# One PSUM pool of seven banks in place of pools of two, two and three, in a decoder-layer kernel on one Trainium2 core

## The chip, the cores and the metric

The kernel runs on one core of a Trainium2 chip. It uses TensorE (PE in the profile), VectorE (DVE), ScalarE (ACT), GpSimd (POOL) and the DMA queue that SyncE (SP) issues. PSUM, into which TensorE writes, is used as eight banks of 128 x 512 floats. The metric is device microseconds of one execution; the time of a kernel is the median of its runs.

## The reference

One inference step of a hybrid decoder layer. For 16 learned meta tokens and 2048 prompt tokens, and for 8 sequences that each decode one token against 4096 cached keys:

```
h = rmsnorm(xp, norm_mix_g)
q, k, v, u = h @ w_in                       # 1024 -> 4 x 512; 8 heads of 64
z = q k^T / 8 + sb_bias                     # strictly causal
a[t,s] = sigmoid(z[t,s]) * prod_{s<j<t} (1 - sigmoid(z[t,j]))
o_attn = a v
o_pool = (windowed means of u over 2, 4, 8, 16 tokens - u) @ pool_w * pool_scale
xp = xp + concat(o_attn, o_pool) @ w_out
xp = xp + (silu(gate) * val) @ w_down       # gate, val: causal conv of width 3 over rmsnorm(xp) @ w_up
y = rmsnorm(xp, norm_final_g)
```

Products of the weights are made to nearly full float precision: each factor is split into a high and a low part, and three products are summed.

## The kernel before

The program has one stretch in which projections and attention run side by side (some 1155 of 2770 us), then the up-projection of the feed-forward network with the decoding mixed in, then the down-projection. Only the first stretch is touched by the change. The pools of PSUM of that stretch are closed before the next one opens its own.

The kernel is written in a framework that records the operations in the order of the Python code and then schedules them: each engine gets its own order, found by list scheduling along a simulated time line, and a semaphore wait for each dependency. A tile is taken from a pool by name; tiles of one tag share the pool's buffers, and a new tile waits until an earlier tile of that tag has been read for the last time. Within one tag tiles get their buffers in the order in which the code asks for them. An engine executes its instructions in its order and cannot overtake a waiting one.

What runs in the first stretch:

- **Preparation** (`prep_first`, `prep_piece`, `turned`): for each of four chunks of 512 tokens, the normalised input is turned by TensorE, four 128 x 128 blocks into one bank (tile `tpx`, L222), and read out by ScalarE and then VectorE into a high and a low part (tile `hk`, L225 and L226), eight such tiles for one chunk.
- **Projections** (`step`, `project`): for each of four groups of 128 columns, four chunks and four kinds (q, k, v, u), 64 in all, a bank is filled by 24 matmuls of 128 x 512 (tile `psm`, L166 to L168) and read out once. k and v are also turned back (tile `pk`, L353). `few_rows` makes the same for the 24 rows of meta and decoded tokens (tiles `t24` and `tq`).
- **Attention** (`attention`): per pair of heads, blocks of 128 queries from the first to the last, and for each block pieces of up to 512 keys from the last backwards. A pair of heads has 45 such units, 180 in all. `chain` makes a unit's scores: per head one bank by two matmuls (tile `z`, L518), which ScalarE reads twice (sigmoid of -z into `om`, L519, of z into `be`, L520). VectorE then scans `om` (L527, L529), and VectorE and GpSimd take turns in multiplying (L534). There are three `om` buffers. `turn` turns the weights, four 128 x 128 blocks to a bank (tile `tt`, L572; the meta columns `ttm`, L582), which ScalarE three times in four and VectorE otherwise copies out (L565; the diagonal by VectorE with a mask, L561), and `weigh` sums their products with the values (tile `po`, L615, a bank of its own).
- **Output** (`out_tile`): with the last pair of heads, each block of 128 tokens is multiplied with w_out: two banks, 24 matmuls each (tile `pso`, L166 to L168), added to the input by VectorE (L687).

The driver (L719 to L733) walks over the 180 units. For each it first calls as many projection steps as are due (`fill_to`), spread evenly over the first three pairs of heads, then `chain` for this unit; after every second unit it calls `weigh` for the two oldest of five pending ones. So in the code's order two units' scores come ahead of the turned weights of units that are three to four older.

Before the change `psm` and `pso` share a pool of two banks, `z` has two, and everything that is turned (`tpx`, `pk`, `tt`, `ttm`, `t24`, `tq` and a few more) shares three; `po` has the eighth.

Of the kernel before, what the change touches and what calls it, by code (L numbers as in the profile page):

```python
# [9 lines left out]
F32 = mybir.dt.float32  # L10
# [6 lines left out]
PSUM = bass.MemoryType.PSUM  # L17
DRAM = bass.MemoryType.DRAM

P = 128  # L20
# [28 lines left out]
CW = 512  # L49
# [12 lines left out]
def hymba_kernel(  # L62
# [100 lines left out]
    def mm3(ps, terms):  # L163
        n = len(terms)
        for i, (ah, al, bh, bl) in enumerate(terms):
            nc.tensor.matmul(ps, ah, bh, start=i == 0, stop=False)  # L166
            nc.tensor.matmul(ps, ah, bl, start=False, stop=False)  # L167
            nc.tensor.matmul(ps, al, bh, start=False, stop=i == n - 1)  # L168
# [3 lines left out]
    main = ctx.enter_context(ExitStack())  # L172
# [9 lines left out]
    for e in range(2):  # L182
        nc.gpsimd.affine_select(out=seen[:, 1, e, :], in_=seen[:, 1, e, :], compare_op=ALU.is_gt, fill=0.0,
                                base=0, pattern=[[1, P]], channel_multiplier=-1)
    psm = main.enter_context(tc.tile_pool(name="ps_mm", bufs=2, space=PSUM, reuse_waits="tile"))
    psz = main.enter_context(tc.tile_pool(name="ps_z", bufs=2, space=PSUM, reuse_waits="tile"))
    pst = main.enter_context(tc.tile_pool(name="ps_t", bufs=3, space=PSUM, reuse_waits="tile"))
    psd = main.enter_context(tc.tile_pool(name="ps_o", bufs=1, space=PSUM, reuse_waits="tile"))
    inp = main.enter_context(ExitStack())
    pa = inp.enter_context(tc.tile_pool(name="pa", bufs=1, side="right", reuse_waits="tile"))  # L190
# [1 line left out]
    def tt_tile(name):  # L192
        return pst.tile([P, 4, P], F32, name=name, tag="tt")

    def room(name):
        return pa.tile([P, META + CW], F32, name=name, tag="kf", bufs=KFB)
# [141 lines left out]
    def window_sums(ub, g, E):  # L338
        src, a = ub, 0
        for st_ in range(g + 1):  # L340
            d = 1 << st_
            a += d
            dst = room("sb")
            nc.vector.tensor_tensor(out=dst[:, a:E], in0=src[:, a:E], in1=src[:, a - d:E - d], op=ALU.add)
            src = dst
        return src
# [3 lines left out]
    def put_tok(dst, g, ch, src):  # L350
        pk = tt_tile("pk")
        for a in range(4):
            nc.tensor.transpose(pk[:, a, :], src[:, a * P:(a + 1) * P], ident)  # L353
        ko = pa.tile([P, 4, P], F32, name="ko", bufs=2)
        nc.scalar.copy(ko, pk)
        t0 = META + CW * ch
        nc.sync.dma_start(out=dst[t0:t0 + CW, g * P:(g + 1) * P].rearrange("(a p) f -> p a f", p=P), in_=ko)

    def project(g, ch, kind, w, hk):
        ps = psm.tile([P, CW], F32, name="psm")  # L360
        mm3(ps, [(w[0][:, c, :], w[1][:, c, :], hk[c][:, 0, :], hk[c][:, 1, :]) for c in range(NK)])
        t0 = META + CW * ch
        kf = room("kf")
        if kind == "u":
            E = META + CW
            nc.vector.tensor_copy(kf[:, 0:META], tails[g])
            nc.scalar.copy(kf[:, META:E], ps)
            if ch < NCH - 1:
                tails[g] = pa.tile([P, META], F32, name="utail", bufs=2)
                nc.vector.tensor_copy(tails[g], kf[:, CW:E])  # L370
            else:
                pk = tt_tile("pku")
                nc.tensor.transpose(pk[:15, 0, :], kf[:, E - 15:E], ident)
                up = pb.tile([P, P], F32, name="up", tag="ot")
                nc.vector.tensor_copy(up[:15, :], pk[:15, 0, :])
                nc.sync.dma_start(out=pool_prompt[:, g * P:(g + 1) * P], in_=up[:15, :])
            src = window_sums(kf, g, E)
            dT = room("dT")
            nc.vector.scalar_tensor_tensor(out=dT[:, 0:CW], in0=src[:, META:E], scalar=1.0 / WIN[g],
                                           in1=kf[:, META:E], op0=ALU.mult, op1=ALU.subtract)  # L380
            nc.sync.dma_start(out=cat_s[4 + g, :, NS + t0:NS + t0 + CW], in_=dT[:, 0:CW])
            return
        kf = kf[:, 0:CW]
        nc.scalar.copy(kf, ps)
        if kind != "v":
            nc.sync.dma_start(out=(q_s if kind == "q" else k_s)[g][:, t0:t0 + CW], in_=kf)
        if kind != "q":
            put_tok(k_prompt if kind == "k" else v_prompt, g, ch, kf)
# [55 lines left out]
    def key_lo(j):  # L444
        return 0 if j == 0 else META + P * (j - 1)

    def attention(hp):
# [55 lines left out]
        def chain(bi, c, top, low):  # L503
            q0, M = (0, META) if bi < 0 else (META + P * bi, P)
            g = bi // 2 if bi >= 0 else -1
            if top:
                st["prev"] = None
            o = q0 - (META + QW * g if g >= 0 else 0)
            qs = slice(o, o + M)
            n = min(key_lo(4 * c + 4), key_lo(bi + 2)) - key_lo(4 * c)  # L510
            be = pb.tile([P, 2, CW], F32, name="be", bufs=BEB)
            om = pb.tile([P, 2, CW + 1], F32, name="om", bufs=OMB)
            nc.gpsimd.memset(om[:M, :, n:n + 1], 1.0)
            for e in range(2):
                h = 2 * hp + e
                z = psz.tile([P, CW], F32, name="z")
                for k in range(2):
                    nc.tensor.matmul(z[:M, :n], qs_[g, e][k][:, qs], kst[c, e][:, 0:n], start=k == 0, stop=k == 1)  # L518
                nc.scalar.activation(out=om[:M, e, 0:n], in_=z[:M, :n], func=AF.Sigmoid, scale=-SCALE, bias=nbias[:M, h:h + 1])  # L519
                nc.scalar.activation(out=be[:M, e, 0:n], in_=z[:M, :n], func=AF.Sigmoid, scale=SCALE, bias=bias[:M, h:h + 1])  # L520
                if bi < 0:
                    nc.gpsimd.affine_select(out=be[:M, e, 0:M], in_=be[:M, e, 0:M], compare_op=ALU.is_gt,
                                            fill=0.0, base=0, pattern=[[-1, M]], channel_multiplier=1)
                rv = om[:M, e, 0:n + 1][:, ::-1]
                if top:
                    hide = unseen[:M, CW - n:CW + 1] if bi >= 0 else unseen[:M, CW - P:CW - P + n + 1]
                    nc.vector.tensor_tensor_scan(out=rv, data0=rv, data1=hide[:, ::-1], initial=1.0, op0=ALU.mult, op1=ALU.max)  # L527
                else:
                    nc.vector.tensor_tensor_scan(out=rv, data0=rv, data1=zero[:M, 0:1].broadcast_to([M, n + 1]),  # L529
                                                 initial=st["prev"][:M, e, 0:1], op0=ALU.mult, op1=ALU.add)  # L530
                m0 = META if low else 0
                if n > m0:
                    cnt["mul"] += 1
                    (nc.gpsimd if cnt["mul"] % 2 == 0 else nc.vector).tensor_tensor(  # L534
                        out=be[:M, e, m0:n], in0=be[:M, e, m0:n], in1=om[:M, e, m0 + 1:n + 1], op=ALU.mult)
            bm = None
            if low:
                bm = pb.tile([P, 2, META], F32, name="bm", bufs=BEB)
                nc.vector.tensor_tensor(out=bm[:M], in0=be[:M, :, 0:META], in1=om[:M, :, 1:META + 1], op=ALU.mult)
            st["prev"] = om  # L540
            return be, bm
# [138 lines left out]
    def out_tile(bi, ch, cl, xt):  # L680
        pc, gffn = out_pool["pc"], out_pool["g"]
        c0, n = TILES[bi + 1]
        for hf in range(2):
            cs = slice(hf * 512, (hf + 1) * 512)
            ps = psm.tile([P, CW], F32, name="pso", tag="psm")
            mm3(ps, [(ch[:, i, :], cl[:, i, :], wo[c][0][:, cs], wo[c][1][:, cs]) for i, c in enumerate(KO)])
            nc.vector.tensor_tensor(out=xt[:, cs], in0=ps, in1=xt[:, cs], op=ALU.add)  # L687
        nc.sync.dma_start(out=xp_s[c0:c0 + n, :], in_=xt)
        xn = pc.tile([P, D], F32, name="xn2")
        r = rstd_of(pc, xt, n, sq=("xn2", 1))  # L690
        nc.vector.scalar_tensor_tensor(out=xn, in0=xt, scalar=r[:, 0:1], in1=gffn, op0=ALU.mult, op1=ALU.mult)
        nc.sync.dma_start(out=h2_s[c0:c0 + n, :], in_=xn)
# [77 lines left out]
    pst = ctx.enter_context(tc.tile_pool(name="pu_t", bufs=1, space=PSUM, reuse_waits="tile"))  # L770
    psm = ctx.enter_context(tc.tile_pool(name="pu_mm", bufs=6, space=PSUM, reuse_waits="tile"))
# [13 lines left out]
    with ExitStack() as es:  # L785
# [216 lines left out]
        for it in range(2 * NF):  # L1002
# [20 lines left out]
            for k in (2 * half, 2 * half + 1):  # L1023
# [15 lines left out]
                for s in range(2):  # L1039
                    fi = f + s * NF  # L1040
                    ps = psm.tile([P, CW], F32, name="psu")
# [24 lines left out]
    with ExitStack() as es:  # L1066
# [130 lines left out]
        for hf in range(2):  # L1197
# [7 lines left out]
            for ti, (a0, n, xc) in enumerate(dt_):  # L1205
# [9 lines left out]
                for q in range(2):  # L1215
                    cs = slice(q * 512, (q + 1) * 512)
                    ps = psm.tile([P, 512], F32, name="psd", tag="psu")
# [35 lines left out]
```

## Time and profile before

| what | value |
|---|---|
| median of three runs | 2768.55 us (2767.65 to 2773.09) |
| the profiled execution | 2771.54 us |
| its span in the trace | 2769.8 us |
| granted TensorE clock over the span | 0.988 |
| first stretch (to the first up-projection) | about 1155 us |
| instructions in the span | 39760 |

The page gives each engine's busy time, a strip of 40 slices of the span, the chain of work that ended last, and the costliest groups of instructions. A busy time counts the union of an engine's instructions. Matmuls overlap in the pipeline, so the duration of one matmul in a row is longer than the distance from its start to the start of the next; costs of TensorE are therefore taken below from starts in the timeline. The table by windows gives each engine's busy time in one stretch of the span.

### The profile page before, as it was taken

To read this page: it belongs to the slowest core of one execution; us is meant where nothing else is said; L and a number is where in the kernel's file an instruction comes from. 1 tells how busy PE (TensorE), PEld (TensorE's weight loads), DVE (VectorE), ACT (ScalarE), POOL (GpSimd) and SP (SyncE) were. 2 spreads that over 40 slices of the span, in tenths; PEclk is the share of its full clock that TensorE was granted. 3 is DMA by queue.
4 is the path that set the end of the run, shared out by engine and by line. 5 is a ranking of instruction groups with operands and counts; after the bars stand their busy time and mean duration, and the time that the engine had idled before them with its cause. 6 is when DMAs were issued, how large, how long until landed. Compare 5 with 4: busy or idle time off the path is not lost.

```text
span 2769.8 us, 39760 instructions
## 1 busy us (share of the span) xinstructions
PE 2662.7 (96%) x14759; PEld 2089.6 (75%) x14759; DVE 1805.2 (65%) x3037; ACT 1031.4 (37%) x1833; POOL 721.7 (26%) x736
## 2 busy tenths in 40 slices
PE   5899999999998999999999999999999999999998
PEld 4677777787786888778877777777776777777776
DVE  4588768857669588669977777777774541114434
ACT  4466656655557256423322222222222320012111
POOL 0012212211122011145554554445554200000000
PEclk9899999999999999999999999999999999999999
DMA  7653552454425433455556555646656574666551
GB/s 252 218 178 118 167 179 97 130 203 136 165 87 171 159 117 101 147 193 193 184 208 242 207 201 213 227 165 237 215 206 237 173 258 165 200 205 212 179 194 64
DMA packets 326375, 498.79 MB, mean 180 GB/s; under 512 B 25367, under 2 KB 238631, under 8 KB 309781
## 3 DMA queue, kind: packets, MB, share of 16 engines
q1 hardware_dynamic: 307749, 362.03, 39.8%
q0 software_dynamic: 18432, 134.23, 12.7%
q8 instruction: 116, 1.90, 0.3%
q14 instruction: 78, 0.64, 0.1%
HBM read 395.99 MB, written 100.59 MB: 179 GB/s over the span
## 4 chain that ended last, share of the span: by engine, by line
PE 79%; DVE 3%; issue 2%; DMA 2%; ACT 1%; POOL 0%; SPq 0%; DVEq 0%; ACTq 0%; POOLq 0%
PE psu L166 12%; PE psu L167 12%; PE psu L168 12%; PE psd L166 6%; PE psd L168 6%; PE psd L167 6%; PE po L615 4%; PE z L518 3%; PE tt L572 3%; PE dav L950 2%; PE psm L166 2%; PE psm L168 2%; PE psm L167 2%; PE pso L167 2%; PE pso L166 2%; PE pso L168 2%
## 5 line engine op out<-in xcount | busy, mean ns | idle before, releaser
L166 PE MATMUL psu<-h2c,uwh 128*128 128x512 f32 x1408 | 555.0, 394 | 4.0 <-ACT uwh L160 2.2
L168 PE MATMUL psu<-h2c,uwl 128*128 128x512 f32 x1408 | 550.7, 391 | 1.3 <-DVE uwl L161 1.3
L167 PE MATMUL psu<-h2c,uwh 128*128 128x512 f32 x1408 | 551.6, 392 | 0.0
L534 POOL TENSOR_TENSOR be<-be,om 128x512 f32<-128x512 f32 (+3 forms) x176 | 182.6, 1037 | 844.2 <-DVE om L529 302.0
L1048 DVE SCALAR_TENSOR_TENSOR cv<-psu,par,cv 128x511 f32<-128x511 f32 x352 | 261.2, 742 | 146.5 <-ACT cv L1045 142.9
L166 PEld LDWEIGHTS psu<-h2c,uwh 128*128 128x128 f32 x1408 | 265.2, 188 | 81.1 <-issue 10.9
L1059 POOL TENSOR_TENSOR cv<-cv,cv 128x512 f32<-128x512 f32 x88 | 224.7, 2554 | 388.6 <-DVE cv L1053 290.7
L168 PEld LDWEIGHTS psu<-h2c,uwl 128*128 128x128 f32 x1408 | 265.3, 188 | 63.7 <-issue 7.3
L167 PEld LDWEIGHTS psu<-h2c,uwh 128*128 128x128 f32 x1408 | 265.3, 188 | 62.1 <-issue 8.5
L529 DVE TENSOR_TENSOR_SCAN om<-om,zero 128x513 f32<-128x513 f32 (+1 forms) x224 | 274.0, 1227 | 46.2 <-ACT om L519 41.2
L519 ACT ACTIVATE om<-z,nbias 128x512 f32<-128x512 f32 (+5 forms) x360 | 213.3, 593 | 138.3 <-PE z L518 83.4
L1045 ACT ACTIVATE cv<-psu,par 128x512 f32<-128x512 f32 x176 | 136.4, 776 | 289.1 <-PE psu L168 289.1
L1220 DVE TENSOR_TENSOR xt<-psd,xt 128x512 f32<-128x512 f32 x64 | 44.0, 691 | 281.8 <-PE psd L168 281.7
L520 ACT ACTIVATE be<-z,bias 128x512 f32<-128x512 f32 (+5 forms) x360 | 211.4, 589 | 0.6 <-PE tt L572 0.6
L167 PE MATMUL psm<-hk,wh 128*128 128x512 f32 x512 | 206.6, 404 | 2.9 <-DVE hk L226 2.9
L166 PE MATMUL psm<-hk,wh 128*128 128x512 f32 x512 | 205.0, 406 | 1.9 <-ACT hk L225 1.3
L168 PE MATMUL psm<-hk,wl 128*128 128x512 f32 x512 | 204.2, 399 | 1.0 <-DVE wl L161 1.0
L161 DVE TENSOR_TENSOR uwl<-uwr,uwh 128x1024 fp32r<-128x1024 f32 x94 | 121.1, 1290 | 127.8 <-ACT uwh L160 127.8
L166 PE MATMUL psd<-wd,ah 128*128 128x512 f32 x512 | 200.3, 395 | 0.0
L167 PE MATMUL psd<-wd,ah 128*128 128x512 f32 x512 | 200.0, 392 | 0.0
L168 PE MATMUL psd<-wd,al 128*128 128x512 f32 x512 | 199.4, 390 | 0.0
L160 ACT CAST uwh<-uwr 128x1024 fp32r<-128x1024 f32 x94 | 98.8, 1054 | 246.4 <-PE psu L167 230.4
(245 smaller groups left out, 4773.8 us busy)
## 6 DMA issues: line engine op xcount, KB each, us to landing
hk<-hs_s SPq DMA_DIRECT2D x96, 512.0 KB
uwr<-in_w_up_dram SPq DMA_DIRECT2D x88, 512.0 KB
act_s<-sg SPq DMA_DIRECT2D x88, 256.0 KB
ar<-act_s SPq DMA_DIRECT2D x32, 704.0 KB
raw<-in_w_up_dram SPq DMA_DIRECT2D x40, 512.0 KB
xt<-in_x_prompt_dram SPq DMA_DIRECT2D x32, 512.0 KB
hs_s<-hk SPq DMA_DIRECT2D x32, 512.0 KB
uwr<-in_w_down_dram SPq DMA_DIRECT2D x22, 512.0 KB
```

Source lines behind the costliest of these rows:

```text
L161: nc.vector.tensor_tensor(out=lo, in0=src, in1=f32(hi), op=ALU.subtract)
L166: nc.tensor.matmul(ps, ah, bh, start=i == 0, stop=False)
L167: nc.tensor.matmul(ps, ah, bl, start=False, stop=False)
L168: nc.tensor.matmul(ps, al, bh, start=False, stop=i == n - 1)
L519: nc.scalar.activation(out=om[:M, e, 0:n], in_=z[:M, :n], func=AF.Sigmoid, scale=-SCALE, bias=nbias[:M, h:h + 1])
L520: nc.scalar.activation(out=be[:M, e, 0:n], in_=z[:M, :n], func=AF.Sigmoid, scale=SCALE, bias=bias[:M, h:h + 1])
L529: nc.vector.tensor_tensor_scan(out=rv, data0=rv, data1=zero[:M, 0:1].broadcast_to([M, n + 1]), initial=st["prev"][:M, e, 0:1], op0=ALU.mul ...
L534: (nc.gpsimd if cnt["mul"] % 2 == 0 else nc.vector).tensor_tensor(out=be[:M, e, m0:n], in0=be[:M, e, m0:n], in1=om[:M, e, m0 + 1:n + 1], o ...
L615: mm = nc.tensor.matmul(o, v_, a_, start=start, stop=stop, skip_group_check=True).ins
L1045: nc.scalar.activation(out=t, in_=ps, func=AF.Identity, scale=cpar(2, fi), bias=cpar(3, fi))
L1048: nc.vector.scalar_tensor_tensor(out=t[:, o:], in0=ps[:, 0:CW - o], scalar=cpar(d, fi), in1=t[:, o:], op0=ALU.mult, op1=ALU.add)
L1059: nc.gpsimd.tensor_tensor(out=cv[1], in0=cv[0], in1=cv[1], op=ALU.mult)
```

## The change

The three pools become one of seven banks with one tag, `tt`. Nothing is computed otherwise, and each engine has the same instructions as before; lines after 185 move up by two.

```diff
-    psm = main.enter_context(tc.tile_pool(name="ps_mm", bufs=2, space=PSUM, reuse_waits="tile"))
-    psz = main.enter_context(tc.tile_pool(name="ps_z", bufs=2, space=PSUM, reuse_waits="tile"))
-    pst = main.enter_context(tc.tile_pool(name="ps_t", bufs=3, space=PSUM, reuse_waits="tile"))
+    pst = main.enter_context(tc.tile_pool(name="ps_t", bufs=7, space=PSUM, reuse_waits="tile"))
...
     def project(g, ch, kind, w, hk):
-        ps = psm.tile([P, CW], F32, name="psm")
+        ps = pst.tile([P, CW], F32, name="psm", tag="tt")
...
-                z = psz.tile([P, CW], F32, name="z")
+                z = pst.tile([P, CW], F32, name="z", tag="tt")
...
-            ps = psm.tile([P, CW], F32, name="pso", tag="psm")
+            ps = pst.tile([P, CW], F32, name="pso", tag="tt")
```

Since all these tiles now have one tag, they get their banks in the order of the code. In the order of TensorE's instructions, the first stretch has 943 tiles besides `po`. Before, 79 of the 96 tiles of projections and output (`psm`, `pso`) get their first matmul while tiles that the code asks for earlier are still to come; now none does, and all 943 are begun in the code's order. After the first stretch TensorE takes the same tiles in the same sequence.

The start of TensorE's order, from the first turned block on (`t_323` and `t_317` are the same tile `t24`, `psm` the projections of q and then k, `pkp` a turn of parameters that are loaded by DMA into `ra`). Before:

```order
L222 MATMUL tpx<-ident,xt 128x128 x12
L166 MATMUL psm<-hk,wh 128x512 x2
L222 MATMUL tpx<-ident,xt 128x128 x4
L167 MATMUL psm<-hk,wh 128x512
L168 MATMUL psm<-hk,wl 128x512
...
L283 MATMUL tps<-ident,xt 128x24 x8
...
L302 MATMUL t_323<-wr,hsml 32x128 x16
L307 MATMUL tq<-ident,sm 128x64
L636 MATMUL pkp<-ident,ra 128x128
```

and now:

```order
L220 MATMUL tpx<-ident,xt 128x128 x32
L281 MATMUL tps<-ident,xt 128x24 x8
L300 MATMUL t_317<-wr,hsml 32x128 x16
L305 MATMUL tq<-ident,sm 128x64
L166 MATMUL psm<-hk,wh 128x512
L167 MATMUL psm<-hk,wh 128x512
L168 MATMUL psm<-hk,wl 128x512
...
L634 MATMUL pkp<-ident,ra 128x128
L635 MATMUL pkp<-ident,rb 128x52
L640 MATMUL pkg<-ident,sp 128x120 x4
```

Before, 48 projection matmuls (q and k) stand between and behind the turned blocks, ahead of `t24` and `pkp`. Now all 32 turned blocks, `t24` and `tq` come first; only the 24 of q stand ahead of `pkp`, and those of k behind `pkg`.

The middle of TensorE's order, in the third pair of heads, where the pool weights of group 2 are folded (`pkf`, `pkw`; the numbers behind `kst`, `qh` and `ql` tell buffers apart). Before:

```order
L572 MATMUL tt<-ident,be 128x128 x8
L395 MATMUL pkf<-ident,pl 128x128
L518 MATMUL z<-kst_6173,qh_6258 128x272
L518 MATMUL z<-kst_6173,ql_6259 128x272
...
L166 MATMUL psm<-hk,wh 128x512
...
L615 MATMUL po<-at,vt 64x128 x16
L518 MATMUL z<-kst_6173,qh_6429 128x400
...
L402 MATMUL pkw<-wt,pT 128x512
```

and now:

```order
L393 MATMUL pkf<-ident,pl 128x128
L613 MATMUL po<-at,vt 64x128 x16
L400 MATMUL pkw<-wt,pT 128x512 x2
L516 MATMUL z<-kst_6167,qh_6252 128x272
L516 MATMUL z<-kst_6167,ql_6253 128x272
...
L570 MATMUL tt<-ident,be 128x128 x14
L580 MATMUL ttm<-ident,bm 32x128
L516 MATMUL z<-kst_6167,qh_6423 128x400
...
```

Before, scores and projections alternate and the first `pkw` has its turn behind 22 projection matmuls; now the code's order holds: `pkf`, `pkw`, one unit's scores, 14 turned blocks, `ttm`, the next unit's scores, and then the 24 matmuls of a projection in one run.

The output part of TensorE's order, at the scores of query block 12 of the last pair of heads. Before:

```order
L572 MATMUL tt<-ident,be 128x128 x7
L518 MATMUL z<-kst_11083,qh_11341 128x256
L518 MATMUL z<-kst_11083,ql_11342 128x256
L572 MATMUL tt<-ident,be 128x128 x4
L518 MATMUL z<-kst_11088,qh_11348 128x256
L518 MATMUL z<-kst_11088,ql_11349 128x256
...
L572 MATMUL tt<-ident,be 128x128 x8
L518 MATMUL z<-kst_10166,qh_11341 128x512
L518 MATMUL z<-kst_10166,ql_11342 128x512
L572 MATMUL tt<-ident,be 128x128 x2
```

and now:

```order
L516 MATMUL z<-kst_11077,qh_11335 128x256
L516 MATMUL z<-kst_11077,ql_11336 128x256
...
L516 MATMUL z<-kst_10165,ql_11343 128x512
L570 MATMUL tt<-ident,be 128x128 x16
L516 MATMUL z<-kst_9487,qh_11335 128x512
...
L570 MATMUL tt<-ident,be 128x128 x6
L613 MATMUL po<-at,vt 64x128 x16
L580 MATMUL ttm<-ident,bm 32x128
L570 MATMUL tt<-ident,be 128x128 x4
```

Before, the two heads' scores of a unit stand apart with turned blocks between them, and further runs of 18 to 21 output matmuls lie between units; now eight score matmuls (two units) stand together, then 16 turned blocks, then the next two units' scores, and 42 of the 48 output matmuls of a block come behind all of these.

## The prediction

> **What bounds the kernel now.** I read the page's shares first, then the strip, then a table by windows, then the waits of TensorE.
>
> ```profile
> span 2769.8 us, 39760 instructions
> PE 2662.7 (96%) x14759; PEld 2089.6 (75%) x14759; DVE 1805.2 (65%) x3037; ACT 1031.4 (37%) x1833; POOL 721.7 (26%) x736
> PE   5899999999998999999999999999999999999998
> PEclk9899999999999999999999999999999999999999
> ```
>
> TensorE is busy for 96% of the span, and at full clock nearly everywhere. What makes the kernel shorter or longer is therefore TensorE's idle time and the cost of its own instructions. Each slice of the strip is 69 us; the idle time sits in the first slices and at a few places behind. The table shows these places (per engine: busy time and instructions, then granted clock, DMA share and rate):
>
> ```profile
> core 0: us, PE busy (x) PEld busy (x) DVE busy (x) ACT busy (x) POOL busy (x), PEclk, DMA share, GB/s
> 20.00:200.00 180.00, 147.32 (x867) 114.28 (x867) 113.39 (x262) 93.15 (x192) 18.79 (x42) 0.91 0.61 206
> 200.00:300.00 100.00, 94.13 (x748) 75.83 (x747) 86.77 (x115) 69.71 (x140) 25.85 (x39) 1.00 0.38 129
> 300.00:460.00 160.00, 156.55 (x1073) 126.08 (x1072) 109.08 (x187) 90.64 (x198) 27.39 (x58) 1.00 0.52 176
> 460.00:540.00 80.00, 71.50 (x549) 54.55 (x548) 68.91 (x102) 55.68 (x115) 24.22 (x38) 0.94 0.33 104
> 540.00:820.00 280.00, 274.88 (x1871) 222.21 (x1870) 190.63 (x299) 153.39 (x323) 47.55 (x95) 0.99 0.44 149
> 820.00:900.00 80.00, 66.85 (x457) 51.88 (x456) 71.90 (x122) 56.40 (x122) 20.78 (x35) 0.96 0.49 151
> 900.00:1155.00 255.00, 254.30 (x1650) 207.14 (x1648) 189.60 (x384) 120.58 (x242) 34.50 (x70) 1.00 0.36 122
> 1155.00:2769.00 1614.00, 1594.78 (x7550) 1235.82 (x7548) 966.16 (x1535) 380.49 (x489) 518.29 (x316) 1.00 0.58 200
> ```
>
> The stretch that the change touches ends at 1155. From 20 to there TensorE is idle for 69.5 us (the difference of length and PE busy, seven windows), 32.7 of them up to 200. In 300 to 460, 540 to 820 and 900 to 1155 (695 us together) it is idle for 9.3 us: there TensorE is the bound, and the projections (or the output) fill its gaps. In 200 to 300, 460 to 540 and 820 to 900 VectorE is busy for 87, 86 and 90%: the scans bound these 260 us, and TensorE idles for 27.5 us. So the question by stage is whether the new order opens gaps in the 695 us, and whether it closes some in the 260.
>
> ```profile
> PE tt L572 <- POOL om L513: 10.3, 6, 2.6
> PE z L518 <- ACT be L520: 8.9, 19, 1.6
> PE pkp L636 <- DMA ra<-in_conv_w_dram: 6.1, 1, 6.1
> PE z L518 <- ACT qh L160: 6.0, 1, 6.0
> PE tt L572 <- DVE at L565: 4.8, 6, 1.2
> ```
>
> These are waits of TensorE by releaser (total, times, longest). Waits for a bank are the second and the fifth: 13.7 us in the whole kernel. A pool that is merely larger has no more than this to give.
>
> **The change part by part.** The multiset of instructions is the same on every engine; what can change is order, waits and the cost that TensorE pays for changing between kinds of matmul.
>
> *Switches.* Turned blocks and `po` are in plain float32, `psm`, `pso` and `z` in another format. Around one switch:
>
> ```profile
> 387.93 0.82 PE L572 MATMUL tt<-ident,be 128*128 128x128 f32 x6
> 388.50 0.48 PE L166 MATMUL psm<-hk,wh 128*128 128x512 f32 x1
> 388.82 0.40 PE L518 MATMUL z<-kst,qh 128*128 128x512 f32 x1
> 389.06 0.39 PE L518 MATMUL z<-kst,ql 128*128 128x512 f32 x1
> 389.29 0.40 PE L167 MATMUL psm<-hk,wh 128*128 128x512 f32 x1
> ```
>
> Six turned blocks take 0.57 from start to start, 0.095 each. The matmul behind them takes 0.32 to the next start, where the following ones take 0.24 and 0.23: a switch costs some 0.09. In TensorE's order of the first stretch such switches fall from 326 to 190, since projections no longer come in pieces between turned blocks: 136 x 0.09 = **-12 us** (0 to -12; at 0 if they lie beside waits).
>
> *Start.* Before, 48 projection matmuls (q and k) lie under the turned blocks, ahead of the wait for `ra`; now `t24` and `tq` come first, then q, then `pkp`, and k behind it.
>
> ```profile
> 22.05 0.73 PE L166 MATMUL psm<-hk,wh 128*128 128x512 f32 x2 [1.31 <-ACT hk L225]
> 35.95 1.06 ACT L209 ACTIVATE sq<-xt 128x1024 bf16<-128x1024 f32 x1 [4.43 <-DMA xt<-in_x_prompt_dram]
> 38.59 0.26 ACT L305 COPY sm<-t 64x128 f32<-64x128 f32 x1 [1.49 <-PE t L302]
> 45.30 0.45 PE L636 MATMUL pkp<-ident,ra 128*128 128x128 f32 x1 [6.12 <-DMA ra<-in_conv_w_dram]
> 45.40 0.77 PE L166 MATMUL psm<-hk,wh 128*128 128x512 f32 x1
> ```
>
> The 24 matmuls of q (24 x 0.233 = 5.6) go into the 6.1 of waiting for `ra`, the 24 of k come behind it, ahead of v, which began at 45.40: 5.6 later, some 7 with the turns of parameters between. `tq` waits for a copy on ScalarE (38.59) that stands behind a load (35.95). The wait of 6.0 of `z` for `qh` can take back a part. I take **+5** (0 if it takes back all, 9 if the copy is late too).
>
> *Preparing the other three chunks.* Now the eight tiles of 32 turned blocks are no longer filled up with matmuls of the next chunk.
>
> ```profile
> L226 DVE SCALAR_TENSOR_TENSOR hk<-tpx,gcol,hk 128x512 fp32r<-128x512 f32 x32 | 23.2, 743 | 16.1 <-ACT hk L225 15.9
> ```
>
> VectorE reads eight tiles in 8 x 0.743 = 5.9 us, TensorE turns them in 32 x 0.095 = 3.0. Three times the difference is 9, if nothing lies in between; scores and `po` do in part. I take **+4** (0 to 9).
>
> *Projections behind scores (300 to 820).* Before, 24 matmuls of a `psm` could start whenever one of its own two banks was free, and TensorE ran them in pieces while ScalarE read `z`. Now a `psm` takes the bank that comes free seventh last in the code's order, and everything behind it on TensorE waits with it: `po`, the next scores, and through them ScalarE and the scans.
>
> ```profile
> 1056.08 0.50 PE L518 MATMUL z<-kst,qh 128*128 128x512 f32 x1
> 1056.90 0.69 ACT L519 ACTIVATE om<-z,nbias 128x512 f32<-128x512 f32 x1 [2.60 <-PE z L518]
> 1057.49 0.68 ACT L520 ACTIVATE be<-z,bias 128x512 f32<-128x512 f32 x1
> 1058.06 0.69 ACT L519 ACTIVATE om<-z,nbias 128x512 f32<-128x512 f32 x1
> ```
>
> ScalarE begins 0.82 after the scores and needs 2 x 0.575 = 1.15 for a bank. Of two units' four `z` the second bank is free some 3.2 after the first score, the third at 4.3, the fourth at 5.4 (0.4 to 0.6 sooner at 400 keys). TensorE is through the scores and 14 turned blocks with `ttm` after 8 x 0.233 + 14 x 0.095 + 0.25 = 3.45. Which bank a `psm` needs follows from the tiles between it and the `psm` before. Counted in the new order: four `z` and four others, 10 times: the second `z`, no wait. Four and five, 13 times: the third, 0.4 as a mean of 512 and 400 keys. Four and six, 6 times: the fourth, less the longer way there, 1.1. Four and seven or eight, 5 times: 1.3 to 1.4. Two projections side by side or behind one unit, 38 times: none. Eight or more `z`, 14 times, mostly where VectorE is the bound: none. The sum is 13 x 0.4 + 6 x 1.1 + 3 x 1.3 + 2 x 1.4 = **+18**. Lower end 0 (TensorE arrives later, because it waited earlier); upper end one read of 0.575 more at each of the 48 places with four or more `z`, +46.
>
> *Output (900 to 1155).* A block of four units takes 21.8 now, first `pso` to first `pso`:
>
> ```profile
> 1046.23 0.40 PE L166 MATMUL pso<-woh,ch 128*128 128x512 f32 x1
> 1068.03 0.39 PE L166 MATMUL pso<-woh,ch 128*128 128x512 f32 x1
> ```
>
> There TensorE is 99.7% busy because `pso` lies between the scores. Now four `z`, four `tt` and the next four `z` follow each other, and 42 of 48 output matmuls come last. The second group's third `z` is reached 8 x 0.233 + 16 x 0.095 + 4 x 0.233 = 4.3 after the first score and takes the bank of the first group's fourth, free at 5.4: 1.1. The fourth and the turned blocks behind take banks whose copies stand behind these reads on ScalarE, which I put at another 0.9. That is 2 for a large block. With six such blocks I take **+12** (-3 if the early scores help VectorE instead, 30 if every one of 12 cycles loses 2.5).
>
> *Stretches bound by VectorE.* The three `om` buffers are not changed, and VectorE has the same scans. I take **0** (-10 to +15).
>
> **Sum:** -12 + 5 + 4 + 18 + 12 + 0 = +27, on the profiled execution's 2771.5: 2798.5. That execution is 3.0 over the median of the runs, so the **forecast is 2795.5** (+1.0%).
>
> **Rivals.**
>
> *A, faster.* If TensorE runs further ahead with scores where VectorE is the bound, the waits for `om`, `be` and `at` in the table of waits (10.3 + 8.9 + 4.8 = 24) can go, and the switches stay won, while the 695 us get no gaps. With half of the waits gone: 2768.5 - 12 - 12 = **2744.5**; with all, 2732.5. For it: 27.5 us of idle TensorE in these 260 us. Against it: VectorE is busy for 86 to 90% there, and `om` still has three buffers. The Trainium skill (Perfetto Trace Analysis, Optimizing Tensor Performance, Matmuls) says that independent groups of matmuls should rotate through different PSUM banks, so that emptying one overlaps the next group; by it seven banks in rotation serve all better than twos and threes. This trace agrees only in so far as the waits for a bank (8.9 and 4.8) exist.
>
> *B, no change.* ScalarE is busy for under 60% of the 695 us; if TensorE arrives at the `psm` late enough, the terms of projections and output are 0, and -12 + 5 + 4 = -3 remains: **2765.5**.
>
> *C, slower still.* The granted clock was 0.91, 0.94 and 0.96 in three of the windows where TensorE idles for over 10%, and 1.00 or 0.99 in the 695 us. If many gaps of about a microsecond bring it to 0.94 there, 686 us of work cost another 686 x 0.06 = 41: **2836.5**. Against it: 1.00 in 200 to 300, with 5.9 us of gaps. The Trainium skill (TensorE: Matmul & The Clock Gate, A second HAM failure mode: psum-queue depth-cycling) tells of a kernel in which cycling through PSUM banks leaves TensorE briefly idle between groups so often that its clock goes up and down; the window of 460 to 540 with 0.94 would fit it, that of 200 to 300 does not.
>
> **How the numbers follow.** The forecast has 0.59, A 0.20, B 0.11, C 0.10. A time within 0.2% of the median (2763 to 2774) is about what a measurement cannot tell from no change. The ends of the terms together give -25 and +97 or so, but they will hardly all fall to one side; the forecast's own range is 2772 to 2835, of which 0.02 may fall into faster and 0.03 into no change. So faster has 0.20 + 0.02 = 0.22, no change 0.11 + 0.03 = 0.14, slower 0.54 + 0.10 = 0.64. The range has to reach A's first time and C's: 2744 to 2844; A's far half and what lies over C's are left out, some 0.15.
>
> **What would show it.** Right: in 300 to 820 waits of `psm` for ScalarE's reads of `z` (`om`, `be`) and for copies of `tt`, together about 18 us, which the trace of before does not have; cycles of about 23.5 in the output; v beginning some 7 us later; less idle time nowhere else. Wrong: if waits of `psm` for a bank sum to under 5 us, the step on projections falls; if the windows bound by VectorE become shorter by 10 us, A holds; if the clock in the 695 us is under 0.97, C. If the stretch after 1155 changes its length, something is moved that I have not seen.

## The result, and the profile after

The changed kernel takes 2882.29 us (median of 3 runs, 2881.5 to 2887.9) against 2768.55: ratio **1.0412, 95% interval 1.0385 to 1.0439**, 114 us slower. The forecast had the sign (+27 us); the size is four times as large, and the time lies over the range.

The page of the changed kernel begins with these lines: span, busy time by engine, and of the strip in 40 slices TensorE's busy share and its granted clock.

```profile
span 2880.6 us, 39721 instructions
PE 2685.0 (93%) x14759; PEld 2111.7 (73%) x14759; DVE 1800.3 (62%) x3037; ACT 1020.8 (35%) x1833; POOL 734.5 (25%) x736
PE   5778889888889899999999999999999999999998
PEclk8889999999999999999999999999999999999999
```

TensorE does the same 14759 matmuls and is busy for 22 us more (2662.7 before); the span is 111 longer. Digits below 9, before only in the first two slices, the thirteenth and the last, now fill most of the first fifteen. To see where, I cut both traces at the same scores. The windows of before (length, busy time by engine, granted clock, DMA share, rate), then those of the changed kernel:

```profile
core 0: us, PE busy (x) PEld busy (x) DVE busy (x) ACT busy (x) POOL busy (x), PEclk, DMA share, GB/s
20.00:201.30 181.30, 148.62 (x875) 115.35 (x874) 114.69 (x263) 93.58 (x193) 19.80 (x43) 0.91 0.61 207
201.30:820.20 618.90, 595.96 (x4228) 477.75 (x4227) 454.08 (x699) 369.00 (x770) 124.09 (x229) 0.99 0.43 146
820.20:1159.70 339.50, 322.33 (x2112) 259.70 (x2110) 266.13 (x518) 181.64 (x372) 55.19 (x103) 0.99 0.40 131
20.00:1159.70 1139.70, 1066.91 (x7210) 852.80 (x7209) 834.91 (x1479) 644.21 (x1335) 199.08 (x374) 0.98 0.45 151
```

```profile
20.00:230.70 210.70, 156.02 (x888) 124.41 (x887) 117.65 (x269) 93.10 (x195) 20.40 (x42) 0.85 0.55 184
230.70:919.20 688.50, 606.04 (x4230) 488.82 (x4229) 447.20 (x693) 361.04 (x769) 127.85 (x230) 0.95 0.38 129
919.20:1269.80 350.60, 326.61 (x2096) 261.16 (x2094) 264.87 (x516) 178.89 (x372) 64.40 (x103) 0.99 0.40 129
20.00:1269.80 1249.80, 1088.67 (x7210) 874.39 (x7208) 829.71 (x1477) 633.03 (x1335) 212.65 (x374) 0.95 0.41 138
```

The whole loss lies in the touched stretch: 1139.7 became 1249.8, +110.1. The first part loses 29.4, the middle 69.6, the last (mostly the output) 11.1. Length less busy time gives TensorE's idle time: 72.8 before, 161.1 now, +88.3; the other 21.8 are busy time, at a clock that fell from 0.98 to 0.95. VectorE and ScalarE are busy for a little less than before, GpSimd for 14 us more, at 17% of the stretch. So nothing new is the bound; TensorE waits more, and works more slowly in between.

Its largest waits in the changed kernel (releaser, total, times, longest; `...` stands for rows left out, three of them for loads and inputs at the start that were there before with nearly the same times):

```profile
PE pkf L393 <- DMA pl<-in_pool_w_dram: 22.1, 3, 10.1
PE pk L351 <- ACT kf L382: 18.0, 19, 3.2
PE tpx L220 <- DVE xp L230: 16.5, 6, 5.8
PE pkw L400 <- DMA wt<-in_w_out_dram: 13.5, 2, 10.1
...
PE po L613 <- DVE at L559: 7.3, 3, 3.9
PE z L516 <- DVE at L563: 7.2, 5, 4.0
...
PE z L516 <- ACT be L518: 4.8, 6, 2.5
PE z L516 <- DVE at L559: 4.5, 4, 2.6
...
PE psm L166 <- DVE at L559: 4.4, 2, 2.4
```

The four costliest rows are not waits for a bank. They are waits of a tile for its **input**: the loads `pl` and `wt` of the fold, the projection's copy `kf` that is turned back, the normalised piece `xp`. `psm` waits little, and scarcely for ScalarE's reads of `z`, on which the forecast had set its largest term. All its matmuls of line 166 in the page's groups (busy, mean ns, then the idle time before them):

```profile
L166 PE MATMUL psm<-hk,wh 128*128 128x512 f32 x512 | 209.8, 410 | 7.6 <-DVE at L559 4.4
```

In the trace of before, the four costliest rows above were:

```profile
PE tpx L222 <- DVE xp L232: 6.0, 4, 2.0
PE pkw L402 <- DMA wt<-in_w_out_dram: 4.9, 2, 4.0
PE pk L353 <- ACT kf L384: 1.3, 1, 1.3
PE pkf L395 <- DMA pl<-in_pool_w_dram: 0.3, 1, 0.3
```

Waits for a bank grew too, though at other tiles than the forecast had: those of `z` sum to 20.2 us over all releasers (8.9 before), three quarters of it for copies of turned weights. Sorted over the whole stretch by whether the work that ended a wait wrote what TensorE reads or read a bank out, waits for an input went from some 40 to some 100 us, waits for a bank from some 20 to some 50.

One such place, the second fold. First the loads before and TensorE before (start, duration, line, operation; in brackets the idle time ahead of it and its releaser):

```profile
362.44 0.80 SPq L596 DMA_DIRECT2D cat_s<-ot  x2
364.01 0.33 SPq L393 DMA_DIRECT2D pl<-in_pool_w_dram  x1
364.40 0.42 SPq L400 DMA_DIRECT2D wt<-in_w_out_dram  x1
```

```profile
361.54 0.51 PE L615 MATMUL po<-atm,vtm 32*64 32x128 f32 x8
361.98 0.45 PE L518 MATMUL z<-kst,qh 128*128 128x400 f32 x1
...
362.80 0.40 PE L166 MATMUL psm<-hk,wh 128*128 128x512 f32 x1
...
365.95 0.30 PE L395 MATMUL pkf<-ident,pl 128*128 128x128 f32 x1 [0.27 <-DMA pl<-in_pool_w_dram]
...
367.10 1.88 PE L402 MATMUL pkw<-wt,pT 128*128 128x512 f32 x4
```

And the same place in the changed kernel, queue of loads and TensorE:

```profile
395.87 5.36 SPq L270 DMA_DIRECT2D hk<-hs_s  x8
402.28 0.93 SPq L594 DMA_DIRECT2D cat_s<-ot  x2
403.30 0.39 SPq L398 DMA_DIRECT2D wt<-in_w_out_dram  x1
404.75 0.32 SPq L379 DMA_DIRECT2D cat_s<-dT  x1
410.21 0.33 SPq L391 DMA_DIRECT2D pl<-in_pool_w_dram  x1
```

```profile
401.34 0.51 PE L613 MATMUL po<-atm,vtm 32*64 32x128 f32 x8
411.98 0.48 PE L393 MATMUL pkf<-ident,pl 128*128 128x128 f32 x1 [10.13 <-DMA pl<-in_pool_w_dram]
412.91 3.78 PE L400 MATMUL pkw<-wt,pT 128*128 128x512 f32 x4 [0.46 <-ACT pT L395]
415.70 1.32 PE L516 MATMUL z<-kst,qh 128*128 128x400 f32 x1
```

In both kernels `pl` is issued within 2 us ahead of `pkf`, behind the `cat_s<-ot` of the products just computed (it shares the buffers of `ot`). Before, TensorE did scores and projections between the products and `pkf`, and waited 0.27. Now the scores and projections behind `pkf` in the code may not take a bank ahead of it, and TensorE stands still for 10.1 us.

The input also comes later than it did. From the end of the last product to `pkf` it took 3.9 us before and takes 10.1 now. `pl` is issued 1.6 us behind `cat_s<-ot` before, 7.9 now: eight loads `hk` of 512 KB each, which were issued 16 us and more ahead of that store before, stand right in front of it, the DMA share from 402 to 410 is 1.01, and the queue waits 4.2 us ahead of `pl` for the store.

Behind that gap TensorE works at half clock. The windows of the gap, of the 6.5 us behind it and of the rest up to 429.1:

```profile
401.90:412.00 10.10, 0.02 (x1) 0.03 (x1) 1.73 (x5) 0.00 (x0) 0.14 (x1) 0.65 0.88 311
412.00:418.50 6.50, 6.04 (x13) 3.50 (x14) 0.70 (x2) 2.72 (x7) 0.00 (x0) 0.50 0.26 94
418.50:429.10 10.60, 10.60 (x69) 8.42 (x68) 6.59 (x13) 5.05 (x14) 1.68 (x4) 1.00 0.14 49
```

The four `pkw` take 3.78 there, against 1.88 at the same place before. The Trainium skill (TensorE: Matmul & The Clock Gate, HAM oscillation — how this bites in real kernels) names idle gaps of TensorE over some 3.4 us as what costs it its clock; at this place the trace agrees, with a gap of 10.1, a clock that falls to 0.50 at 404.9, 3.0 us into it, and stays there until 418.5. Elsewhere it does not need so long a gap: behind a single wait of 1.9 us that ends at 725.1 the clock is 0.50 from 725.7 to 729.2. Here the measurement decides.

### The profile page after: what moved, and what is told of

It reads as the page before. It is cut to its first block, busy times and chain, and to the rows that moved or that the text cites. A ratio compares the mean times of both kernels' runs of the same rounds, so it can differ in the third digit from the quotient of the medians.

```text
span 2880.6 us, 39721 instructions
## 1 busy us (share of the span) xinstructions
PE 2685.0 (93%) x14759; PEld 2111.7 (73%) x14759; DVE 1800.3 (62%) x3037; ACT 1020.8 (35%) x1833; POOL 734.5 (25%) x736
## 4 chain that ended last, share of the span: by engine, by line
PE 61%; DVE 3%; issue 1%; ACT 1%; DMA 1%; SPq 0%; POOL 0%; ACTq 0%; DVEq 0%
PE psu L166 11%; PE psu L167 11%; PE psu L168 11%; PE psd L166 5%; PE psd L168 5%; PE psd L167 5%; PE dav L948 2%; PE pso L166 2%; PE pso L167 2%; PE pso L168 2%; PE po L613 1%; PE few L1138 1%; PE fewd L1109 1%; PE z L516 0%; DMA uwr<-in_w_down_dram 0%
## 5 line engine op out<-in xcount | busy, mean ns | idle before, releaser
L532 POOL TENSOR_TENSOR be<-be,om 128x512 f32<-128x512 f32 (+3 forms) x176 | 198.1, 1125 | 935.7 <-DVE om L527 366.0
L1043 ACT ACTIVATE cv<-psu,par 128x512 f32<-128x512 f32 x176 | 136.5, 776 | 287.8 <-PE psu L168 287.7
L518 ACT ACTIVATE be<-z,bias 128x512 f32<-128x512 f32 (+5 forms) x360 | 217.6, 605 | 0.0
```

The lines of the kernel that those rows point to most:

```text
L1043: nc.scalar.activation(out=t, in_=ps, func=AF.Identity, scale=cpar(2, fi), bias=cpar(3, fi))
```

## The experiments

Theory ORDER (numbers 1 to 6): with one tag, TensorE begins all tiles in the code's order, and the oldest tile whose input is late stops everything; the number of banks does not matter. After number 3 had missed by this, it became WINDOW (from number 7 on): TensorE also goes at most as many tiles ahead as there are banks. The main rival, BANKS: seven banks shared by all are too few. WINDOW takes a part of BANKS in. Ratios are to the kernel before, run beside each; the changed kernel has 1.0412. Diffs are against the changed kernel unless said otherwise.

**1. The fold's tiles apart (six shared, one for pkf and pkw).**

```diff
-    pst = ...(tc.tile_pool(name="ps_t", bufs=7, ...))
+    pst = ...(tc.tile_pool(name="ps_t", bufs=6, ...))
+    psl = ...(tc.tile_pool(name="ps_x", bufs=1, ...))
...
+        if name in ("pkf", "pkw"):
+            return psl.tile([P, 4, P], F32, name=name, tag="late")
```

> One bank of the seven is set apart for the tiles pkf and pkw (the folding of the pool weights), six are shared. Theory ORDER (with one tag every tile is begun in the code's order, so a tile whose input comes late holds up all work behind it): the waits of pkf and pkw for their loads (22.1 and 13.5 us in the changed kernel) are filled with other work, and the half clock behind them goes: 2882 - 36 - 10 = about 2836 us (2824 to 2850), waits of TensorE for pl and wt under 5 us. Theory BANKS (the shared banks are too few): one bank less for everything else, 2890 us or more. Theory CLOCK-first (the lower clock is the cause, gaps are secondary): 2870 or more.

Measured: 2874.81 us, **1.0379** (1.0362 to 1.0396). A miss for ORDER and for BANKS; the time lies in the range of CLOCK-first. Against that theory stands number 10, where 51 us are gone at an unchanged clock of 0.95. The waits of number 1 for the fold:

```profile
PE pkf L396 <- DMA pl<-in_pool_w_dram: 2.1, 1, 2.1
PE pkw L403 <- DMA wt<-in_w_out_dram: 1.0, 1, 1.0
```

The waits went, as ORDER says, but the time fell by 9 us only. Either they had cost little, or the bank that was taken away cost nearly as much as they. Number 3 decides that.

**2. All turned tiles but the attention weights apart (five shared, two apart).** `tt_tile` draws on a pool `psl` of two banks, `pst` has five.

> Two banks are set apart for all that is turned except the attention weights (tpx, tps, t24, tq, pk, pku, pkp, pkg, pkf, pkw), five are shared by scores, attention weights, projections and output. Theory ORDER: besides the fold's waits those of tpx (16.5 for xp) and pk (18.0 for kf) are filled: 2882 - 36 - 30 - 15 = about 2800 us (2785 to 2820), idle time of TensorE in the first stretch under 100 us (158.7 in the changed kernel, 69.5 before). Theory BANKS: 2900 us or more.

Measured: 2891.47 us, **1.0443** (1.0425 to 1.046). A miss again, and again two things were changed at once.

**3. Six banks, one tag** (`bufs=6`, nothing else).

> One pool and one tag as in the changed kernel, but with six banks, the seventh unused. Theory ORDER: the order of the tiles stays, 2882 us within 12. Theory BANKS: waits for banks grow clearly, 2910 us or more.

Measured: 2908.48 us, **1.0499** (1.0481 to 1.0516), a miss for ORDER and much nearer to BANKS. One bank less costs 0.0087, some 24 us. It is the control that number 1 lacked: at six shared banks, setting the fold apart brings 1.0499 down to 1.0379, some 33 us. So both effects exist and nearly cancelled in number 1.

**4. Projections and output apart (two banks, five shared).** `psm` and `pso` draw on a pool of two of their own.

> Projections and output (psm, pso) have a pool of two banks again, scores and everything turned share five. Theory ORDER: TensorE can do projections while a tile of the other pool waits for its input, as before: 2778 us (2765 to 2795), idle time in the first stretch under 90 us. Rival (that scores and turned tiles share banks is what costs): 2830 us or more.

Measured: 2801.82 us, **1.0112** (1.0095 to 1.0129), somewhat over the range of ORDER, far below the rival's. The banks are seven as in the changed kernel, but three quarters of the loss are gone.

**5. Scores apart (two banks, five shared).** `z` draws on a pool of two of its own.

> The scores z have two banks of their own again, projections, output and everything turned share five. Theory ORDER: projections and turned tiles stay in the code's order among themselves, so the waits for pl, wt, xp and kf stop all of them; only scores can fill, and those are few: 2850 us (2825 to 2880). Rival (that scores share banks with the rest is what costs): 2790 us or less.

Measured: 2825.27 us, **1.0197** (1.018 to 1.0214), at the lower end of ORDER's range. Scores fill gaps too, some seven tenths as well as projections (0.0215 against 0.03).

**6. Earlier loads for the fold.** `pl` and the first half of `wt` get buffers of their own and are loaded three steps earlier.

```diff
+    def fold_loads(g):
+        pl = pa.tile([P, P], F32, name="pl")
...
+        wt = pa.tile([P, CW], F32, name="wt")
...
+        if (ch, ki) == (1, 0):
+            fold_loads(g)
```

> One pool of seven as in the changed kernel; the loads of pl and of the first half of wt go into buffers of their own and are asked for three projection steps earlier. Theory ORDER: the waits for pl (22.1) and for the first wt go, the second wt may still wait: 2882 - 30 - 8 = about 2844 us (2830 to 2862), with the banks unchanged. Theory BANKS: 2882 us within 10, since the same waits turn up at another tile.

Measured: 2892.36 us, **1.0438** (1.0421 to 1.0456): no gain, near what BANKS expects. But its waits show why it does not decide:

```profile
PE pkw L408 <- DMA wt<-in_w_out_dram: 31.6, 4, 12.5
PE pkw L408 <- ACT pT L402: 11.4, 2, 9.0
```

`pkf` no longer waits for `pl`, but `pkw` waits for the rest of the loads. The edit did not make the inputs early; number 9 does it by leaving the loads out.

**7. Five banks, one tag** (`bufs=5`), the control for number 2.

> One tag with five banks, as control for the kernel that shares five and has two apart for late tiles (ratio 1.0443). Theory WINDOW (TensorE can only go as many tiles ahead in the code's order as there are banks, and stops at the oldest tile whose input is late): from seven to six the ratio went from 1.0412 to 1.0499; to five at least as much again, 1.060 or more, so that setting late tiles apart is worth 1.6% or more at five banks. If it is under 1.050, late tiles cost little and the banks decide by themselves.

Measured: 2987.2 us, **1.0787** (1.0769 to 1.0805). As WINDOW expected. With five banks for the rest, setting the late tiles apart (number 2, which uses two banks more) is worth 0.034. The price of a bank rises: 0.009 from seven to six, 0.029 from six to five.

**8. k and v turned back behind the next scores**, in the code's order:

```diff
     def put_tok(dst, g, ch, src):
+        late.append(lambda: turn_back(dst, g, ch, src))
...
         pend.append((h, h[2](*un), un))
+        flush()
```

> One pool of seven as in the changed kernel; the turning back of k and v (pk) is written behind the next unit's scores instead of directly behind the projection, so that its copy kf has been made by then. Theory WINDOW: the waits of pk for kf (18.0 us, 19 times) fall to under 4 us and the time by 12 to 25 us, ratio 1.033 to 1.037. If the waits only move to other tiles, the ratio stays within 1.039 to 1.044.

Measured: 2863.53 us, **1.0335** (1.0318 to 1.0353). No pool, no bank and no instruction is changed, only the place in the code, and 21 us are gone. The wait of `pk` did not quite fall to the 4 us expected. Its row, 18.0 in the changed kernel:

```profile
PE pk L360 <- ACT kf L391: 5.5, 8, 1.8
```

**9. The fold without loads** (`pl` is the identity, `wt` the high part of the normalised input).

> One pool of seven as in the changed kernel; the folding of the pool weights takes the identity in place of pool_w and the high part of the normalised input in place of the rows of w_out, so its twelve loads are left out and its output is another. Theory WINDOW: the waits for pl and wt (22.1 and 13.5 us) go and the half clock behind them, 36 + 8 = 44 us less: 2838 us, ratio 1.025 (1.019 to 1.031). If the waits move to other tiles: 1.036 or more.

Measured: 2850.15 us, **1.03** (1.0279 to 1.032), in the range of WINDOW: 31 us of the 44 expected, while the number of banks is the same.

**10. Both.**

> Both: the fold takes inputs that are there already (its twelve loads left out, output another), and k and v are turned back behind the next unit's scores. Theory WINDOW: the gains add, ratio 1.012 to 1.024. If the waits move to other tiles: 1.034 or more.

Measured: 2833.18 us, **1.0226** (1.0209 to 1.0243): 51 us together, where the single gains are 21 and 31. They add, so these waits did not merely move elsewhere. Its stretch, from 20 to the first up-projection:

```profile
20.00:1222.00 1202.00, 1083.30 (x7209) 876.85 (x7207) 829.21 (x1477) 630.69 (x1335) 203.65 (x374) 0.95 0.43 142
```

TensorE is still idle for 118.7 (72.8 before), and the clock is still 0.95.

**11. Both, and projections apart (two and five).**

> Projections and output have two banks of their own, the rest share five; besides, k and v are turned back behind the next scores, and the fold takes inputs that are there already (its twelve loads left out, output another). Theory WINDOW: what was left of 63 us in the kernel with both edits alone is projections that can't run past waiting tiles of attention; with a pool of their own they do, and the late inputs of the turned tiles (pk 9.5, pkf 3.9, pkw 2.4 us of waiting where projections alone were apart) go as well: ratio 1.004 (1.000 to 1.010). Rival (the rest is the start and the preparation of the chunks, tpx for xp, which a pool for projections doesn't touch): 1.015 or more.

Measured: 2791.41 us, **1.007** (1.0056 to 1.0084), as WINDOW expects. Some two thirds of the remainder of number 10 are thus room for projections to fill. Against number 4 (1.0112) the two edits bring only 0.004: once projections can fill, these late inputs cost little.

**12. A fourth pool in the kernel before** (against the kernel before: of the three banks for turned tiles, one for all but `tt` and `ttm`).

> The kernel before with one more division: projections and output two banks, scores two, attention weights (tt, ttm) two, everything else that is turned one. Theory WINDOW: attention weights no longer wait behind tiles with late inputs, and these no longer behind attention weights; but the waits for banks of tt (4.8 for copies, in the kernel before) grow with one bank less: 0.998 (0.993 to 1.004). If dividing were better in itself: under 0.993. If the bank that tt loses decides: over 1.004.

Measured: 2805.88 us, **1.0126** (1.0111 to 1.0141). A miss for WINDOW: more division does not help. The time lies where it was expected if the bank that `tt` loses decides, and the largest wait is one for such a bank, held by the diagonal's copy on VectorE (0.5 before). But the edit also leaves the other turned tiles one bank instead of three, and TensorE is idle for only 12.6 us more in a stretch that is 33.5 longer; what each part costs was not tried apart.

```profile
PE tt L573 <- DVE at L562: 14.3, 9, 6.2
```

**13. One bank for projections and output, six shared.**

> Projections and output have one bank of their own, six are shared by scores and turned tiles (with two and five the ratio was 1.0112). If it matters that projections are a line of their own, one bank holds most of it: 1.010 to 1.020, the loss at each projection being its readout of 0.6 to 1 us that scores and turned tiles can fill. If it is the number of banks that projections have: 1.030 or more.

Measured: 2826.35 us, **1.0208** (1.0194 to 1.0222), between the two cases: half of the loss is gone with a line of their own of a single bank, and the second bank (number 4, 1.0112) brings another 0.0096.

**14. Turned tiles apart (three banks); scores, projections and output share four.**

> Scores, projections and output share four banks; everything turned has three of its own, as before. Theory WINDOW in its narrow form (what costs is sharing a line with tiles whose inputs come late: turned weights that wait for scan and product, tpx for xp, pk for kf, the fold for its loads; scores and projections have inputs that lie ready): 1.002 (0.996 to 1.008). In its wide form (projections must be free of scores too, since a score that waits for its bank holds them): 1.012 to 1.020.

Measured: 2791.77 us, **1.0079** (1.0065 to 1.0093), the upper end of the narrow form. Its stretch, from 20 to the first up-projection:

```profile
20.00:1179.30 1159.30, 1071.74 (x7211) 861.03 (x7209) 837.08 (x1479) 636.78 (x1335) 210.50 (x374) 0.97 0.45 149
```

Idle 87.6, clock 0.97. Four fifths of the loss are gone with one boundary: that between the turned tiles, whose inputs are computed or loaded shortly before, and the scores and projections, whose inputs lie ready. The attention weights belong on the first side by this run and by number 2, which left them with the scores and stayed at 1.0443. Whether they cost by their late inputs or by holding banks for which `z` waits (20.2 us in the changed kernel) is not shown; `tt` itself waits there for some 2 us for inputs. No version tried beats the kernel before.

## Why the forecast was too small

**What held.** The sign, and that the loss arises because projections no longer fill gaps. The last part, with the output, was put at +12 and lost 11.1, but that is luck: over five full blocks, from the last addition of one to that of the next, it takes 109.3 us before and 112.6 now, 0.7 a block where 2 was forecast. The rest was lost ahead of these blocks. That VectorE's stretches bring neither gain nor loss of their own cannot be told apart in the windows, but VectorE's busy time did not change (834.9 and 829.7).

**The step that failed** is the term for projections behind scores, +18. It asked when the bank of a `psm` comes free, and found ScalarE's reads of `z` as what ends last. The waits of `psm` are 7.6 us in all, most of it for VectorE's copies, and not the 18 that the forecast wanted to see, though more than the 5 below which it wanted to give the step up; yet the middle lost 69.6. I had written that everything behind a waiting `psm` waits with it, and did not apply the same sentence to the tiles that wait for an *input*. The fold and the turning back of k and v had no term in the sum. Before, such waits cost TensorE little (1.3 for `kf`, 0.3 for `pl`, 4.9 for `wt`) because it did something else meanwhile. The table of waits shows a wait after the cover has been subtracted; with the order fixed, the cover goes, and the latency itself has to be priced: from the code's neighbours of each such tile, how long after the last work ahead of it its input arrives. For the fold a part of the price was visible: in the trace of before `pkf` begins 3.9 us behind the last product. The other part was not, since the new order also moved the loads `hk` in front of the store on which `pl` waits. Numbers 8, 9 and 10 show that `pk` cost 21 us and the fold 31. Waits for a bank did come in the middle, 7.6 at `psm` and 18.5 at `z` (5.6 before), which is not far from the 18 of the term. But most of them are for copies of turned weights and not for ScalarE's reads of `z`, so that agreement is luck as well.

**The start and the preparation** were put at +5 and +4; this part lost 29.4. v begins at 61.56, 16 us later than before, where some 7 was forecast: the matmuls of q were to go into the wait for `ra`, but `tq` waits longer, `ra` comes 3 us later, and `pkp` still waits 6.0 for it. The wait of 16.5 for `xp` (6.0 before), all but 2.8 of it up to 214, is the same oversight as in the middle: I priced what VectorE takes to read eight tiles, not that all of TensorE stands until VectorE has multiplied the piece. It was not tried apart.

**The clock** was a rival of its own (C, 0.94 in the middle, +41, chance 0.10), to come from many gaps of about a microsecond. It came, 0.95 in the middle and 0.85 in the first part; each fall in the changed kernel's stretch has a gap of 1.7 us or more just ahead of it, the longest 10.1. So it is a part of the same loss, and belonged into the forecast as soon as gaps were expected. Its price isn't isolated by a run, but the trace gives an estimate: added up over the stretches at clock 0.50, TensorE was busy for 41.8 us before and for 89.4 now. At full clock that work would take about half, so the clock costs some 24 us more. That accounts for all of the 21.8 more of busy time and leaves the 136 fewer switches some 2 us, where the forecast took 12.

**The ends of the terms** come to +109 and not +97, since the switches had 0 as their upper end; the measured +114 lies beyond even this, so some cost had no term. And the 13.7 us of waits for a bank were the two largest rows; with the small ones there were some 20.

**Rival A** (faster) and **B** (no change) fell. The Trainium skill (Perfetto Trace Analysis, Optimizing Tensor Performance, Matmuls) has matmul groups rotate through different banks; seven in rotation gave 1.0412, three and four 1.0079, two, two and three 1.0. Rotation was not what was lacking here.

**Open** are the last 0.008 of number 14, in which scores and projections still share a line, the price of `xp` by itself, and how much of the loss is due to banks that the attention weights hold.

## What to carry to other kernels

Tiles that share a tag share an order, if buffers are given out as the code asks for them: the number of banks is then how far the engine may run ahead, and the tile with the latest input sets the pace of all. Put tiles whose inputs lie ready and tiles whose inputs have just been computed or loaded in different pools, so that the first can fill while the second wait. And when a change takes away freedom of order, do not price it by the waits that the old trace shows: these are what was left after filling; price the latencies behind them.

## What the runs showed of the hardware that was not expected

The cost of waiting has a tail: 3.0 us into a gap of 10.1 us TensorE's granted clock fell to 0.50, it stayed there for 6.5 us behind the gap, and four matmuls of 128 x 512 took 3.78 us instead of 1.88. Every stretch at 0.50 between 20 us and the first up-projection lasts 3.4 us or two, three or four times as long; there are 20 of them in the changed kernel, 136.5 us together, and 10 before, 54.6. Over the stretch the clock fell to 0.95 with 161.1 us of idle time, was 0.97 with 87.6 (number 14), and 0.98 with 72.8.
